# Pools divided by last reader at the two late joints of a hybrid layer, row splits placed among o-projection tiles, and later groups combined on VectorE

## The chip, the cores and the metric

The kernel runs on one core of a Trainium2 chip. The metric is the device time of one execution, in microseconds (us). A core has TensorE (PE), which multiplies matrices into banks of PSUM, VectorE (DVE), ScalarE (ACT) and GpSimd (POOL), each with its own instructions in its own order, and DMA queues that move data between the core's SBUF and the device memory. Engines wait for each other only through semaphores.

## The reference

One layer of a hybrid streaming trunk, for 17 tiles of 128 rows (16 of the prompt, one with eight short streams) and a width of 1024:

```
h   = rmsnorm(x, norm_mix_pre);   P = h @ w_in                    # 1024 x 3592
mix = concat(gated_delta_rule(conv(P[qkv])) * silu(P[z]), P[B] * conv(P[C] * P[H]))
x   = x + rmsnorm(mix @ w_o, norm_mix_post)
h   = rmsnorm(x, norm_ffn_pre)
f   = (silu(h @ w_gate) * (h @ w_up)) @ w_down                    # 1024 x 2816, 2816 x 1024
x   = x + rmsnorm(f, norm_ffn_post)
```

Besides x the layer returns the new convolution caches and the states of the delta rule.

## The kernel before, in words

All products are in fp32, in three passes: each operand is split into a high part that the TensorE format holds exactly and a low part (`xh`/`xl` for the rows, `fw` for gate/up weights, `as` and `dw` in the down projection), and high·high, high·low and low·high are summed in PSUM. A split is a cast on ScalarE (the high part) and a subtraction on VectorE or GpSimd (the low part).

The program has five stages. The **projections** with the delta rule end at about 1028 us. The **o-projection** (`o_tile`, one call for each of 17 tiles) ends at about 1247 us: it loads a tile of mixed rows `mr` and of x (`xo`), splits `mr` into `mh` and `ml`, issues 48 matmuls against `woh`/`wol`, normalizes, adds, normalizes again into `hx` (L731), transposes `hx` with 8 transposes on TensorE (L737), scales them into `ht` (L738) and writes `ht` to the device memory as `hTd` (L741), from where the next stage reads it back.

The **gate/up stage** does 7 products of half-size blocks in place of 8, as Strassen's scheme does. Its rows are in three groups (`FGROUPS`: 6, 6 and 5 tiles). For a group, `ffn_load` reads the row blocks B11 to B22, `ffn_sums` and `ffn_prep` form the combinations T1 to T4 on VectorE and split all seven parts (`PARTS`, four blocks of depth each: 28 casts at L849, 28 subtractions at L850). Before the change the subtractions alternate between VectorE and GpSimd, one for one. Then come 22 rounds, one for each block of 128 hidden columns. A round has weights in seven forms (`gu_weights`, splits at L894 and L895; in group 0 they are computed and mostly stored, later groups load four of the seven), four first products into four PSUM banks (`gu_start`), and `gate_up`: ScalarE copies three banks out into `m1`, `m7`, `m5` (L955 to L957), three further products are added into the banks, VectorE and GpSimd combine them (`u`, `c`, `s7`; L963 to L970), ScalarE applies silu (L966, L971), VectorE multiplies (L983, L984), and every second round ScalarE's queue issues the DMAs that store the six parts for the down projection (`partd`, L995; `lastd`, L987).

The **down projection** runs over five chunks of the hidden columns and eight pairs of row tiles and a single one. `split` (L1059, L1062) prepares `as`, `down_chunk` (L783, L785) prepares `dw`, `product` issues the matmuls (L1078), `evac` and `acc_add` (L1099, L1037) move banks into accumulators. In the last chunk `finish` takes the sum of squares (L1087), the reciprocal root (GpSimd, L130), multiplies by it and by `gpo` (L1092), adds x (L1093) and stores (L1095).

Where code is written in the program order, a list scheduler in the framework decides the order of each engine's instructions from a model of their times. Memory is given out by pools. A pool that is opened over the place of a closed one makes the first writers of its tiles wait for the last readers of what lay there. Around the change the pools are: `op` (all of the o-projection), `fs` (rows of group 0 on load), `fe` (raw weights `rg`, `ru`, sums, 2 split-weight buffers), `fb` (10 more, and the tiles of the epilogue), `fp` (split rows), `fd` and `dr` (loads for the next group, and for the down projection), `dn` (the whole of the down projection). `issue_after` lets a DMA be issued only after a named earlier one. `O_SPLIT` is the number of o tiles that are written ahead of group 0's row splits. Two split weights of the first round lie in closed `woh` tiles (`early`), so that `gu_start` of the first round is written ahead of the closing of `op`.

## Time and profile before

| | |
|---|---|
| median of 3 runs | 2676.9 us (2676.51 to 2684.25) |
| the profiled execution | 2681.64 us, its span 2679.8 us |
| TensorE busy | 2540.3 us, 95% |
| VectorE, ScalarE, GpSimd busy | 1698.4, 945.5, 895.1 us |
| mean granted TensorE clock | 0.976 of full speed |

The span is the time from the first to the last recorded instruction. Busy times can overlap and matmul ends are modelled. A share of busy time is an average over stages with different limits, so the places where TensorE stands idle matter, not the sum. The joints between the stages are at 1152 to 1164 us (row splits of group 0 amid the o-projection), 1256 to 1268 us (o-projection to group 0), 1588 to 1596 us (group 0 to 1), 1912 to 1932 us (group 1 to 2) and 2190 to 2202 us (group 2 to the down projection).

### The profile page before, as it was taken

How to read it: one execution, taken by the hardware profiler on the slowest of the kernel's cores; microseconds unless marked ns; L12 is line 12 of the kernel's file. 1: busy time of each engine (PE TensorE's matmuls, PEld its weight loads, DVE VectorE, ACT ScalarE, POOL GpSimd, SP SyncE). 2: the span in 40 equal slices, each digit the busy share in tenths (PEclk: the TensorE clock that was granted, in tenths of full speed). 3: DMA queues.
4: the chain of work that ended last, by engine and by line, in shares of the span. 5: the costliest groups of instructions: out<-in, count | busy, mean ns of one | idle time of the engine just before them, and what ended most of it. 6: DMA issues, size and time to landing. Idle time of an engine off the chain costs nothing.

```text
span 2679.8 us, 42128 instructions
## 1 busy us (share of the span) xinstructions
PE 2540.3 (95%) x15105; PEld 2358.5 (88%) x15105; DVE 1698.4 (63%) x3405; ACT 945.5 (35%) x2278; POOL 895.1 (33%) x820
## 2 busy tenths in 40 slices
PE   5789999999999999999999999999899999999997
PEld 4679989899898997878999999999899987887775
DVE  7877656576665755586888873433633344777698
ACT  3424134151431513343433442222332335333343
POOL 2221001010000101132655664444544445555563
PEclk8889999999999999999999999999999999999999
DMA  8887655656656565666987777887888853433365
GB/s 297 299 299 264 231 200 197 231 193 217 232 192 218 191 221 173 199 229 211 327 271 268 268 268 251 261 267 243 278 278 277 274 168 109 125 124 120 125 215 175
DMA packets 320241, 602.02 MB, mean 225 GB/s; under 512 B 56876, under 2 KB 206064, under 8 KB 298528
## 3 DMA queue, kind: packets, MB, share of 16 engines
q1 hardware_dynamic: 191728, 522.99, 57.8%
q10 hardware_dynamic: 128304, 76.34, 9.3%
q8 instruction: 119, 1.95, 0.3%
q14 instruction: 90, 0.74, 0.1%
HBM read 437.19 MB, written 162.05 MB: 224 GB/s over the span
## 4 chain that ended last, share of the span: by engine, by line
PE 38%; DVE 6%; issue 2%; POOL 2%; DMA 1%; ACT 1%; ACTq 0%; DVEq 0%; POOLq 0%; SPq 0%
PE fbank L919 28%; PE fbank L1078 10%; DVE xl L850 1%; DVE acc L1037 1%; DVE xr L1093 1%; DVE acc L1092 1%; DMA dr<-in_w_dn 1%; POOL dw L785 1%; DMA fh<-hTd 0%; POOL as L1062 0%; ACTq L995 0%; DVE acc L1125 0%; DVE dw L785 0%; POOL f2r L130 0%; DVE as L1062 0%
## 5 line engine op out<-in xcount | busy, mean ns | idle before, releaser
L919 PE MATMUL fbank<-xh,fw 128*128 128x384 f32 (+1 forms) x3696 | 904.4, 328 | 19.5 <-ACT m L955 10.9
L136 PE MATMUL dbank<-hi,w 128*128 128x384 f32 (+1 forms) x2688 | 705.8, 341 | 33.6 <-ACT w L296 10.4
L919 PEld LDWEIGHTS fbank<-xh,fw 128*128 128x128 f32 x3696 | 655.8, 189 | 22.3 <-ACT m L955 12.4
L919 PE MATMUL fbank<-xl,fw 128*128 128x384 f32 (+1 forms) x1848 | 604.8, 327 | 0.0
L136 PEld LDWEIGHTS dbank<-hi,w 128*128 128x128 f32 x2688 | 494.1, 197 | 47.3 <-ACT w L296 12.0
L1078 PE MATMUL fbank<-dw,as 128*128 128x512 f32 x1980 | 463.9, 395 | 13.0 <-ACT dw L783 4.9
L1078 PEld LDWEIGHTS fbank<-dw,as 128*128 128x128 f32 x1980 | 372.5, 189 | 104.2 <-DVE acc L1037 7.3
L136 PE MATMUL dbank<-lo,w 128*128 128x384 f32 (+1 forms) x1344 | 454.0, 338 | 0.0
L919 PEld LDWEIGHTS fbank<-xl,fw 128*128 128x128 f32 x1848 | 349.3, 189 | 0.0
L136 PEld LDWEIGHTS dbank<-lo,w 128*128 128x128 f32 x1344 | 264.5, 197 | 2.3 <-issue 0.2
L1062 POOL TENSOR_TENSOR as<-ar,as 128x256 fp32r<-128x256 f32 (+1 forms) x207 | 187.6, 916 | 174.2 <-ACT as L1059 170.6
L895 POOL TENSOR_TENSOR fw<-rg,fw 128x512 fp32r<-128x512 f32 x124 | 176.2, 1421 | 181.3 <-ACT fw L894 180.9
L1037 DVE TENSOR_TENSOR acc<-acc,fbank 128x512 f32<-128x512 f32 x248 | 166.5, 682 | 98.7 <-PE fbank L1078 83.1
L1059 ACT CAST as<-ar 128x256 fp32r<-128x256 f32 (+1 forms) x288 | 118.1, 427 | 182.9 <-PE fbank L1078 139.0
L894 ACT CAST fw<-rg 128x512 fp32r<-128x512 f32 x124 | 77.4, 624 | 183.4 <-PE fbank L919 136.9
L508 POOL MEMSET AU<- 32x128 f32 x16 | 3.1, 194 | 409.3 <-PE gbank L494 401.9
L323 DVE SCALAR_TENSOR_TENSOR acc<-R,cw,acc 128x384 f32<-128x384 f32 (+1 forms) x216 | 129.9, 605 | 1.6
L964 POOL TENSOR_TENSOR m<-m,m 128x384 f32<-128x384 f32 (+1 forms) x66 | 69.6, 1055 | 158.3 <-ACT m L957 113.3
L895 POOL TENSOR_TENSOR fw<-ru,fw 128x512 fp32r<-128x512 f32 x62 | 92.4, 1490 | 83.5 <-ACT fw L894 69.0
L963 DVE TENSOR_TENSOR u<-m,fbank 128x384 f32<-128x384 f32 (+1 forms) x66 | 34.8, 528 | 134.4 <-PE fbank L919 127.9
L968 DVE TENSOR_TENSOR c<-u,fbank 128x384 f32<-128x384 f32 (+1 forms) x66 | 34.9, 528 | 127.4 <-PE fbank L919 127.3
L467 DVE TENSOR_TENSOR pr<-As,Ts 48x87 f32<-48x87 f32 (+21 forms) x186 | 64.8, 349 | 30.9 <-DMA As<-sa 26.2
(309 smaller groups left out, 3692.8 us busy)
## 6 DMA issues: line engine op xcount, KB each, us to landing
w<-wsplit SPq DMA_DIRECT2D x140, 1024.0 KB, 4.9
fw<-fsplit SPq DMA_DIRECT2D x188, 512.0 KB, 4.7
fsplit<-fw SPq DMA_DIRECT2D x94, 512.0 KB, 5.3
partd<-pt ACTq DMA_DIRECT2D x88, 384.0 KB, 7.2
rg<-in_w_gu SPq DMA_DIRECT2D x62, 512.0 KB, 3.7
wsplit<-w SPq DMA_DIRECT2D x28, 1024.0 KB, 5.4
ar<-partd SPq DMA_DIRECT2D x48, 384.0 KB, 3.4
ar<-partd SPq DMA_DIRECT2D x64, 256.0 KB, 2.7
```

The lines of the kernel that those rows point to most:

```text
L136: T.matmul(ps, l, r, start=(i == 0), stop=(i == n - 1))
L323: V.scalar_tensor_tensor(acc, raw(d), w[:, d:d + 1], acc, op0=ALU.mult, op1=ALU.add)
L467: V.tensor_mul(p3, As[:m, j, j + 1:32].unsqueeze(2).broadcast_to([m, a, b]), Ts[:m, j, 0:b].unsqueeze(1).broadcast_to([m, a, b]))
L894: A.copy(w[:, 0], v)
L895: e.tensor_tensor(out=w[:, 1], in0=v, in1=w[:, 0].bitcast(F32), op=ALU.subtract)
L919: T.matmul(ps, w_[:, c], b_[k][:, :hw], start=(first and k == 0 and ci == 0), stop=(k == KH - 1 and ci == 2), skip_group_check=not first)
L964: G.tensor_tensor(out=s7, in0=s7, in1=s5, op=ALU.add)
L968: V.tensor_add(c21, u2, b3)
L1037: V.tensor_add(dst, dst, ps)
L1059: ins = A.copy(a[:, 0, :n], v)
L1062: e.tensor_tensor(out=a[:, 1, :n], in0=v, in1=a[:, 0, :n].bitcast(F32), op=ALU.subtract)
L1078: T.matmul(ps, a[:, x_, q * P:(q + 1) * P], w[:, y_], start=(start and q == 0 and ci == 0), stop=(q == c - 1 and ci == 2), skip_group_chec ...
```

## The change

It has six parts.

1. `O_SPLIT` goes from 14 to 8 and `ffn_prep` becomes a generator that yields after each of the seven parts: in program order, group 0's splits of one part are followed by one o tile, seven times, and three o tiles come after.
2. At the joint to group 0, `op` is divided: `oa` holds what the matmuls of the o-projection read (`woh`, `wol`, `mr`, `mh`, `ml`), `op` what the rest of a tile needs. `oa` is closed first and `fb` is opened over it. The two early weights and the early `gu_start` are gone. `NWE`, the weights in `fe`, goes from 2 to 4, and `rg`/`ru` alternate between one buffer in `fe` and one in `fb`.
3. At the joint to the down projection `dn` is divided: `da` (`as`, `ar` and 12 of the `dw` buffers) and `dn` (accumulators and the rest).
4. Groups 1 and 2: the first sums of T2 are computed earlier, with the others (`t2` tiles), and VectorE takes all work that GpSimd had in these rounds: the splits of rows, the splits of three weights (a11, a12, a22) and two additions to `s7`. In group 0 GpSimd keeps one row split of four (`k == 0`).
5. In group 2 the first loads for the down projection (`dr`, `ar0`) are issued after a weight load of that round.
6. `finish` multiplies by `gpo` before the reciprocal root is known, then does one multiply-and-add; for the last tile half of the squares go to VectorE, and its last evacuations get high priority.

```diff
-O_SPLIT = 14
+O_SPLIT = 8
-NWE = 2
+NWE = 4
+NDQ = 12
...
         op = ps_o.enter_context(tc.tile_pool(name="op", bufs=1, reuse_waits="tile", side="right"))
+        oa = ps_a.enter_context(tc.tile_pool(name="oa", bufs=1, reuse_waits="tile", side="right"))
...
-            wh = op.tile([P, D], F32R, name=f"woh{k}")
-            wl = op.tile([P, D], F32R, name=f"wol{k}")
+            wh = oa.tile([P, D], F32R, name=f"woh{k}")
+            wl = oa.tile([P, D], F32R, name=f"wol{k}")
...
-                nc.sync.dma_start(out=t, in_=w_dn[f])
+                with tc.issue_after(wl[0].ins) if not dring else ExitStack():
+                    nc.sync.dma_start(out=t, in_=w_dn[f])
...
-            pool, b = (dr, NDR) if n % NDW < NDR else (dn, NDW - NDR)
+            m = n % NDW
+            pool, b = (dr, NDR) if m < NDR else (da, NDQ) if m < NDR + NDQ else (dn, NDW - NDR - NDQ)
...
+                if gi:
+                    t2.append(fs.tile([P, HW], F32, tag="t2", name="ft2", bufs=KH)[:, :hw])
+                    V.tensor_sub(t2[k], b22, b12)
+                else:
+                    t2.append(b12)
+            return t3, t2
...
-                    (V if k % 2 else G).tensor_tensor(
+                    (G if k == 0 and not gi else V).tensor_tensor(
                         out=l[:, :hw], in0=v, in1=h[:, :hw].bitcast(F32), op=ALU.subtract)
...
-            return X
+                yield X
...
-            hid = ffn_prep(0, hs, ffn_sums(0, hs, fs))
+            prep = ffn_prep(0, hs, ffn_sums(0, hs, fs))
+            for t in range(O_SPLIT, O_SPLIT + len(PARTS)):
+                hid = next(prep)
+                o_tile(t)
...
+            e0 = V if gi else G
...
-            for i, (v, e) in enumerate(((a11, G), (s[2], V), (s[0], G), (s[1], V), (a12, G), (a22, G), (s[3], V))):
+            for i, (v, e) in enumerate(((a11, e0), (s[2], V), (s[0], G), (s[1], V), (a12, e0), (a22, e0), (s[3], V))):
...
-        early += ["woh0", "woh1"]
-        ffetch(2)
-        started = gu_start(0, 0, hid)
+        ps_a.close()
+        fb = ph.enter_context(tc.tile_pool(name="fb", bufs=1, reuse_waits="tile"))
         ps_o.close()
-        fb = ph.enter_context(tc.tile_pool(name="fb", bufs=1, reuse_waits="tile"))
...
-            G.tensor_tensor(out=s7, in0=s7, in1=s5, op=ALU.add)
+            (V if gi else G).tensor_tensor(out=s7, in0=s7, in1=s5, op=ALU.add)
...
-            G.tensor_tensor(out=s7, in0=s7, in1=u2, op=ALU.add)
+            (V if gi else G).tensor_tensor(out=s7, in0=s7, in1=u2, op=ALU.add)
...
+        da = ph.enter_context(tc.tile_pool(name="da", bufs=1, reuse_waits="tile"))
         dn = ph.enter_context(tc.tile_pool(name="dn", bufs=1, reuse_waits="tile"))
...
-                A.activation(junk, v[:, h], AF.Square, accum_out=ss[:, h:h + 1])
+                if h and tail:
+                    V.scalar_tensor_tensor(junk, v[:, h], 1.0, v[:, h], op0=ALU.mult, op1=ALU.mult, accum_out=ss[:, h:h + 1])
+                else:
+                    A.activation(junk, v[:, h], AF.Square, accum_out=ss[:, h:h + 1])
...
             for h in range(2):
+                V.tensor_mul(v[:, h], v[:, h], gpo[:, 512 * h:512 * h + 512])
+            for h in range(2):
                 c = slice(512 * h, 512 * h + 512)
-                V.scalar_tensor_tensor(v[:, h], v[:, h], r, gpo[:, c], op0=ALU.mult, op1=ALU.mult)
-                V.tensor_add(xt[:, c], xt[:, c], v[:, h])
+                V.scalar_tensor_tensor(xt[:, c], v[:, h], r, xt[:, c], op0=ALU.mult, op1=ALU.add)
```

In the built order every engine's instructions are the same up to the o-projection. Three places follow; a row is a line, an operation, its output and input, the shape and a count, and line numbers of the change differ from those of before by 2 to 16 (L860 is L850 of before, L733 is L731).

VectorE in the o-projection, around `hx` of tile 7, which TensorE transposes next. Here `xl` is a low part of a row split, `fh` a row block or a sum of blocks, `oym`, `oxm` and `oss` belong to the norms of o tiles, and `ml` to the split of the next tile. Before:

```order
L128 TENSOR_SCALAR oym<-oss 128x1
L850 TENSOR_TENSOR xl<-ft_12623,xh 128x384
L833 TENSOR_TENSOR fh<-fh 128x384
L850 TENSOR_TENSOR xl<-fh,xh 128x384 x3
L843 TENSOR_TENSOR fh<-fh 128x384
L850 TENSOR_TENSOR xl<-ft_12629,xh 128x384
L731 TENSOR_SCALAR hx<-xo,oyr 128x1024
L843 TENSOR_TENSOR fh<-fh 128x384
L850 TENSOR_TENSOR xl<-fh,xh 128x384
L719 TENSOR_TENSOR oss<-oss 128x1
L709 TENSOR_TENSOR ml<-mr,mh 128x512
```

and with the change:

```order
L129 TENSOR_SCALAR oym<-oss 128x1
L721 TENSOR_TENSOR oss<-oss 128x1
L860 TENSOR_TENSOR xl<-fh,xh 128x384
L711 TENSOR_TENSOR ml<-mr,mh 128x512
L860 TENSOR_TENSOR xl<-fh,xh 128x384
L711 TENSOR_TENSOR ml<-mr,mh 128x512
L853 TENSOR_TENSOR fh<-fh 128x384
L129 TENSOR_SCALAR oxm<-oss 128x1
L853 TENSOR_TENSOR fh<-fh 128x384
L733 TENSOR_SCALAR hx<-xo,oyr 128x1024
L855 TENSOR_TENSOR fh<-fh 128x384
L853 TENSOR_TENSOR fh<-fh 128x384
```

The splits stand in one cluster in both orders (50 rows long before, 58 with the change) and not over seven tiles. VectorE has 21 of the 28 subtractions in place of 14. From the first of them to this `hx` there are 27 rows before and 39 with the change.

ScalarE at the joint of groups 1 and 2. `m` is a bank copied out (L955 to L957 before, L966 to L968 with the change), `c` the silu input, `partd` the stores of the six parts, `fw` a split weight. Before:

```order
L966 ACTIVATE m_19453<-fbank 128x384
L849 CAST xh<-fh 128x320 x9
L971 ACTIVATE c_19456<-c_19456 128x384
L955 COPY m_19643<-fbank 128x320
L956 COPY m_19644<-fbank 128x320
L995 DMA partd_4_117<-pt 128x6x128 x3
L957 COPY m_19645<-fbank 128x320
L894 CAST fw<-rg 128x512
```

and with the change:

```order
L859 CAST xh<-ft_18820 128x320
L859 CAST xh<-fh 128x320 x2
L966 COPY m_19655<-fbank 128x320
L982 ACTIVATE c_19472<-c_19472 128x384
L967 COPY m_19656<-fbank 128x320
L968 COPY m_19657<-fbank 128x320
L907 CAST fw<-rg 128x512
L1006 DMA partd_4_117<-pt 128x6x128 x3
L977 ACTIVATE m_19716<-fbank 128x320
```

The first copy stands ahead of the silu, the third copy and the weight cast ahead of the three stores. All 28 subtractions of this joint are VectorE's, and GpSimd has none.

ScalarE at the joint of group 2 and the down projection. `as` and `dw` are the first operands of it, `ar` and `dr` their sources, `acc` an evacuated bank. Before:

```order
L971 ACTIVATE c_22553<-c_22553 128x320
L987 DMA lastd_127<-pt 128x64
L995 DMA partd_4_122<-pt 128x6x128 x2
L1099 COPY acc_0_22579<-fbank 128x512
L1059 CAST as<-ar 128x256
L783 CAST dw<-dr 128x512 x2
```

and with the change:

```order
L982 ACTIVATE c_22565<-c_22565 128x320
L998 DMA lastd_127<-pt 128x64
L1071 CAST as<-ar 128x256
L787 CAST dw<-dr 128x512 x2
L1071 CAST as<-ar 128x256
L787 CAST dw<-dr 128x512 x2
L1071 CAST as<-ar 128x256
L787 CAST dw<-dr 128x512 x2
L1071 CAST as<-ar 128x256 x2
```

The first casts stand ahead of the stores and of the evacuation, and seven or more of them go before the first evacuation.

On TensorE, at the joint to group 0, 38 o matmuls, 9 product matmuls, 8 transposes, 77 product matmuls and 8 transposes follow each other with the change, where it was 12 o matmuls, 8 transposes, 36 product matmuls and 8 transposes before. In the o-projection 103 o matmuls (up to two tiles ahead) precede the transposes of `hx` above, where it was 79.

More of the change, by code (lines that the diff above doesn't have):

```diff
@@ L753, in fbank @@
         return pool.tile([P, 512], F32, tag=tag, name="fbank")
-    dring, dprep, cast = {}, [], []
+    dring, dprep, cast, wl = {}, [], [], []
     def down_chunk(ch):
@@ L827, in ffn_sums @@
             hw = len(FGROUPS[gi]) * P // 2
-            t3 = []
+            t3, t2 = [], []
             for k in range(KH):
@@ L929, in gu_start @@
             return banks
-        for t in range(O_SPLIT, NT):
+        for t in range(O_SPLIT + len(PARTS), NT):
             if t == NT - 1:
@@ L1002 @@
             if gi:
-                hid = ffn_prep(gi, hs, t3)
+                *_, hid = ffn_prep(gi, hs, t3)
             if gi + 1 < len(FGROUPS):
@@ L1079, in product, with finish @@
                              stop=(q == c - 1 and ci == 2), skip_group_check=True)
-        def finish(v, places):
+        def finish(v, places, tail=False):
             xt = dr.tile([P, D], F32, tag="dr", name="xr", bufs=4)
@@ L1143, in down_single @@
             product(b2, ch, a2, 6, False)
-            evac(c1, b1, ch)
-            acc_add(c2, b2)
-            if ch == len(FCHUNKS) - 1:
+            end = ch == len(FCHUNKS) - 1
+            with tc.high_priority() if end else ExitStack():
+                evac(c1, b1, ch)
+                acc_add(c2, b2)
+            if end:
                 r1, r2 = rows(u)
-                finish(acc[u], [(0, r1), (64, r2)])
+                finish(acc[u], [(0, r1), (64, r2)], True)
         pairs = [(gi, j) for gi, g in enumerate(FGROUPS) for j in range(len(g) // 2)]
```

39 lines of the change are left out of this document (19 added, 20 removed).

## The prediction

> **What bounds the kernel now.** I read the page's totals first, then tables of time windows around each change of stage, then the timeline inside those windows.
>
> ```profile
> span 2679.8 us, 42128 instructions
> PE 2540.3 (95%) x15105; PEld 2358.5 (88%) x15105; DVE 1698.4 (63%) x3405; ACT 945.5 (35%) x2278; POOL 895.1 (33%) x820
> ```
>
> TensorE is busy for 95% of the span, and the change leaves its matmuls as they are. What can be won is the time in which TensorE stands still or runs at a lower granted clock. The windows show where that lies (columns: window in us, its length, busy us and count for each engine, granted TensorE clock, DMA share, GB/s).
>
> ```profile
> core 0: us, PE busy (x) PEld busy (x) DVE busy (x) ACT busy (x) POOL busy (x), PEclk, DMA share, GB/s
> 1152.00:1156.00 4.00, 0.57 (x3) 0.14 (x1) 4.00 (x6) 2.05 (x5) 3.38 (x3) 0.99 0.00 0
> 1156.00:1164.00 8.00, 6.35 (x22) 5.41 (x23) 7.56 (x15) 3.04 (x6) 4.30 (x3) 0.58 0.39 123
> 1256.00:1260.00 4.00, 0.43 (x4) 0.19 (x2) 1.72 (x3) 2.23 (x5) 1.54 (x2) 0.79 0.41 115
> 1260.00:1268.00 8.00, 8.00 (x33) 8.00 (x34) 6.52 (x7) 5.27 (x11) 8.00 (x6) 0.68 0.96 332
> 1588.00:1592.00 4.00, 0.43 (x3) 0.11 (x1) 4.00 (x6) 2.08 (x6) 2.27 (x2) 1.00 0.43 131
> 1592.00:1596.00 4.00, 3.72 (x13) 3.72 (x14) 3.32 (x7) 0.70 (x2) 0.00 (x0) 0.60 0.02 7
> 1912.00:1916.00 4.00, 1.81 (x12) 1.55 (x12) 3.71 (x7) 1.11 (x3) 1.13 (x2) 1.00 0.84 261
> 1916.00:1924.00 8.00, 3.13 (x22) 2.87 (x20) 1.75 (x4) 0.15 (x1) 0.00 (x0) 1.00 1.00 368
> 1924.00:1932.00 8.00, 7.01 (x30) 7.01 (x31) 4.93 (x7) 4.74 (x12) 6.47 (x6) 0.58 0.63 202
> 2190.00:2194.00 4.00, 1.06 (x5) 0.56 (x3) 2.14 (x4) 1.43 (x4) 0.46 (x1) 0.95 0.40 115
> 2194.00:2202.00 8.00, 7.42 (x20) 5.58 (x21) 7.47 (x6) 5.03 (x12) 8.00 (x7) 0.60 0.46 143
> 1264.00:1570.00 306.00, 301.99 (x1732) 300.26 (x1731) 250.06 (x295) 124.50 (x252) 185.95 (x128) 1.00 0.83 289
> 1600.00:1888.00 288.00, 288.00 (x1664) 288.00 (x1663) 108.21 (x147) 80.19 (x159) 120.30 (x101) 1.00 0.81 255
> ```
>
> The two long windows, inside groups 0 and 1, have TensorE full at clock 1.00: nothing can be won there. Each joint loses twice, by idle time and by a low clock just behind it. I count idle as length less PE busy, and clock as PE busy times (1 − clock):
>
> - amid the o-projection: 3.43 + 1.65 idle, 6.35 × 0.42 = 2.67 clock, 7.75 together
> - into group 0: 3.57 idle, 8 × 0.32 = 2.56 clock, 6.1
> - group 0 to 1: 3.57 + 0.28 idle, 3.72 × 0.40 = 1.49 clock, 5.3
> - group 1 to 2: 2.19 + 4.87 + 0.99 = 8.05 idle, 7.01 × 0.42 = 2.9 clock, 11.0
> - into the down projection: 2.94 + 0.58 idle, 7.42 × 0.40 = 2.97 clock, 6.5
>
> That is 36.7 us in five places, the ceiling of the joints. The tail behind the last matmul comes on top.
>
> **The change part by part.** *Amid the o-projection.*
>
> ```profile
> 1156.76 0.74 DVE L731 TENSOR_SCALAR hx<-xo,oyr 128x1024 f32<-128x1024 f32 x1
> 1157.65 1.94 PE L737 MATMUL ftbank<-cst,hx 128*128 128x128 f32 x8 [5.08 <-DVE hx L731]
> ```
>
> TensorE's transposes wait 5.08 us for `hx`, behind a VectorE that is full (4.00 of 4.00): its queue holds the subtractions of the splits. How dear one is depends on GpSimd:
>
> ```profile
> 1577.47 0.55 DVE L843 TENSOR_TENSOR fh<-fh 128x384 f32<-128x384 f32 x1
> 1577.94 1.38 DVE L850 TENSOR_TENSOR xl<-fh,xh 128x384 fp32r<-128x384 f32 x1
> 1577.71 2.48 POOL L850 TENSOR_TENSOR xl<-fh,xh 128x384 fp32r<-128x384 f32 x2 [2.57 <-ACT xh L849]
> ```
>
> Alone such an operation takes 0.55, beside a GpSimd one 1.38, so each subtraction on GpSimd costs VectorE up to 0.83. The change moves 7 of them: VectorE gets 7 × 0.55 = 3.9 more of its own and loses up to 7 × 0.83 = 5.8 of delay. That is 2 better at most on VectorE. Against it, `hx` stands 12 rows later in the cluster; for it, TensorE has 24 more o matmuls ahead of the transposes, at the 6.35 / 22 = 0.29 of the second window some 7 us of cover. The spreading over seven tiles did not happen in the built order. I take 2; bounds −2 (VectorE later, cover used by the rows) to 7.75.
>
> *Into group 0.* The weights of the first round could not be cast until the last tile was through:
>
> ```profile
> 1257.77 0.62 ACT L894 CAST fw<-rg 128x512 fp32r<-128x512 f32 x1 [4.56 <-DVE ht L738]
> ```
>
> ScalarE waits 4.56 us, in order, behind the DMA issue that needs `ht`; TensorE stands 3.57. With `fb` over `oa` alone, these casts and the bank copies need only the o matmuls, and the order has them ahead of that issue; 86 product matmuls fill what 36 did. Against it, round 1's weights are now needed sooner than they are split, since GpSimd is full (8.00 of 8.00) and so are the DMAs (0.96). I put a rest of 1.5 us down for that: 6.1 − 1.5 = 4.6; bounds 2 (a rest as long as today's wait, its clock saved) to 6.1.
>
> *Group 0 to 1.*
>
> ```profile
> 1591.34 0.52 ACT L971 ACTIVATE c<-c 128x384 f32<-128x384 f32 x1 [1.22 <-DVE c L970]
> 1591.77 0.46 ACT L955 COPY m<-fbank 128x384 f32<-128x384 f32 x1
> ```
>
> The bank copy that TensorE waits for is behind a silu, which is behind the `c` addition on a VectorE that is full of splits. In the new order the copy goes first and GpSimd no longer doubles VectorE's operations. The wait goes whole: 5.3; bounds 3.9 (idle only) to 5.3. The later silu is covered by four products.
>
> *Group 1 to 2.* The same wait (2.19) and then a larger one:
>
> ```profile
> 1917.45 6.96 ACTq L995 DMA_DIRECT2D partd<-pt  x3
> 1924.51 0.43 ACT L957 COPY m<-fbank 128x320 f32<-128x320 f32 x1 [8.36 <-issue]
> ```
>
> The third copy stands behind three DMA issues that took 6.96 us while the DMAs were full (share 1.00, 368 GB/s). The change puts copy and weight cast ahead of them, and moves the first 2 MB of down weights to later in the group. What is late next is the first silu behind those issues; its banks are wanted after one product of a round. If the issues still take 7 us, a part comes back. 11.0 less 1.5 = 9.5; bounds 3 (the 2.19, and little more) to 11.0.
>
> *Into the down projection.*
>
> ```profile
> 2191.55 0.97 ACTq L995 DMA_DIRECT2D partd<-pt  x2
> 2194.03 0.80 PE L1078 MATMUL fbank<-dw,as 128*128 128x512 f32 x1 [2.97 <-ACT dw L783]
> ```
>
> TensorE waits 2.97 us for a `dw` cast that stands behind those stores and an evacuation. Now the casts come first, about 2.7 us sooner. But part of the `da` buffers lie over split rows that the last product of group 2 reads, and the low parts behind the casts (GpSimd full, 8.00 of 8.00 in the next window) are unchanged. I take 4 of the 6.5; bounds 0 to 6.5.
>
> How short must a rest be to leave the clock alone? The wait of 2.19 us was followed by a window at 1.00, that of 2.97 by one at 0.60; so I charge no clock to a rest of 1.5. The Trainium skill ("TensorE: Matmul & The Clock Gate", "What's actually happening") halves the clock after an idle window of about 3.4 us, which runs free of the kernel. By that rule the wait of 2.97 could go without a loss, and this last term would be about 2.7 in place of 4, the sum 25.5; the trace shows the loss, so the row decides.
>
> *Tail.*
>
> ```profile
> 2667.53 1.42 DVE L1092 SCALAR_TENSOR_TENSOR acc<-acc,f2r,gpo 128x512 f32<-128x512 f32 x2
> 2668.86 0.68 DVE L1093 TENSOR_TENSOR xr<-xr,acc 128x512 f32<-128x512 f32 x1
> 2669.46 0.68 DVE L1037 TENSOR_TENSOR accs<-accs,fbank 128x512 f32<-128x512 f32 x1
> 2670.24 0.63 ACT L1087 ACTIVATE junkd<-accs 128x512 bf16<-128x512 f32 x1 [5.79 <-DVE accs L1037]
> 2672.82 1.41 DVE L1092 SCALAR_TENSOR_TENSOR accs<-accs,f2r,gpo 128x512 f32<-128x512 f32 x2 [0.73 <-POOL f2r L130]
> 2674.15 1.29 DVE L1093 TENSOR_TENSOR xr<-xr,accs 128x512 f32<-128x512 f32 x2
> ```
>
> Two squares in parallel save about 0.75 (0.63 and its readout). Behind the root stood 1.41 + 1.29 = 2.70; now it is one pass of 1.41, and before it the 1.41 − 0.73 = 0.68 of the multiplication by `gpo` that the wait does not hold: 0.6 less. The last addition, ahead of other tiles' 1.42 + 0.68, can come up to 2.1 sooner, of which I count half. 0.75 + 0.6 + 1.05 = 2.4; bounds 0.5 to 4.
>
> *Costs.* In group 0 VectorE (250.06 of 306) gets four T2 sums for group 1: 4 × 0.55 to 4 × 1.38, 2.2 to 5.5 if nothing hid them; I take −1, bounds −5.5 to 0. In group 1, GpSimd's 101 operations (five a round, at 7 products × 12 = 84 matmuls a round 1664 / 84 = 19.8 rounds) go to VectorE: two of five at 0.55, three on 512 columns at 0.55 × 512/384 = 0.73, about 66 us; 108.21 + 66 = 174 of 288. TensorE's 288.00 hides it: 0. Without that cover it would be 3.3 us a round.
>
> Sum: 2 + 4.6 + 5.3 + 9.5 + 4 + 2.4 − 1 = 26.8. The profiled execution would take 2681.6 − 26.8 = 2654.8. That execution lies 4.7 above the median, so the median goes from 2676.9 to about 2650.
>
> **The rivals.**
>
> *Half of it.* The two joints that depend on VectorE and GpSimd both (amid the o-projection, into group 0) and the down joint give nothing: the first since its splits stay clustered, the others since the split of the next weights ends last anyway. Then 5.3 + 9.5 − 1 + 0.6 of the tail remain, 14.4: about 2662. For it speak GpSimd's full windows behind both joints; against it, that the waits shown end with a ScalarE cast and not with a low part.
>
> *All of it.* Every joint closes and the 24 more o matmuls hide `hx`: 36.7 + 2.4 less 3 of rest, 36, about 2641. Against it speaks the cluster.
>
> *It doesn't do what it says.* Memory decides when loads and splits start, not the readers named: each joint finds another wait of the same length. DMA share 1.00 and the full VectorE are for this; that four of five waits end with a ScalarE instruction placed behind something else is against. Within 8 us of 2676.9.
>
> *Slower: VectorE's order.* With all the work of a later round on VectorE, a subtraction that waits for its ScalarE cast holds the additions behind it, which free the banks.
>
> ```profile
> 2164.81 1.25 DVE L984 TENSOR_TENSOR pt<-m,c 128x320 f32<-128x320 f32 x1 [0.61 <-ACT c L971]
> ```
>
> VectorE already waits for ScalarE (0.61) in a round. It decides when bank readers come later by more than TensorE's run of products, about four of a round's seven: a round is 288 / 19.8 = 14.5 us, so some 8 us. One us over that, in 44 rounds, is 44 us: 2650 + 44 = 2694. Against it: VectorE has 6 us of 14.5 to spare even with the 3.3 more.
>
> **How the numbers follow.** The forecast (2643 to 2657 with its own bounds) gets 0.50, half of it 0.26, all of it 0.11, no effect 0.08, slower 0.05. The joint bounds sum to far more on both sides but won't fall on one side together. The range from 2638 to 2667 takes in the forecast, all, and nearly all of the half case. About 0.3%, 8 us, is what a measurement of this kernel can tell from no change: faster 0.87, same 0.08, slower 0.05.
>
> **What would show it.** Right: the window at the joint of groups 1 and 2 has under 2 us idle and no row in which a bank copy waits for "issue" for several us; group 0 to 1 has no wait of TensorE for the first copy (L966 by then); clock at both stays at 1.00; GpSimd has no busy time in groups 1 and 2, VectorE about 174 of 288, TensorE still 288.00; the last operation on VectorE ends about 2.4 sooner behind the last evacuation's bank than now. Amid the o-projection I expect a wait for `hx` still, of 2 to 5 us. Wrong: TensorE idle inside the rounds of groups 1 and 2; a new wait of TensorE for a low part (`fw` or `dw`) at the start of group 0 or of the down projection; or silu behind stalled stores in group 2's first round.

## The result, and the profile after

The changed kernel takes 2652.99 us (median of 4 runs, 2650.85 to 2655.23), against 2677.15 us before: a ratio of 0.9904, with a 95% interval from 0.9888 to 0.9919. On a second chip the same kernel had 2651.63 against 2682.42 us, 0.9878 (0.9860 to 0.9896). The forecast was 2650, in a range from 2638 to 2667.

The page of the profiled execution (2650.85 us) begins so:

```profile
span 2649.1 us, 41837 instructions
PE 2527.0 (95%) x15105; PEld 2350.1 (89%) x15105; DVE 1755.8 (66%) x3650; ACT 945.3 (36%) x2276; POOL 610.5 (23%) x577
```

TensorE has the same 15105 matmuls and has 13.3 us less of busy time, since it no longer runs at a low clock behind the joints. GpSimd's busy time fell by 285 us.

Single runs of one kernel lie 4 to 12 us apart, about as much as one joint is worth. A sharper measure is how long each stage takes inside a profile, from the first matmul of one stage to that of the next. On the timeline of TensorE, before:

```profile
1028.14 0.47 PE L714 MATMUL dbank<-woh,mh 128*128 128x512 f32 x1
...
1245.74 0.34 PE L919 MATMUL fbank<-xh,fw 128*128 128x384 f32 x1
...
2188.15 0.63 PE L1078 MATMUL fbank<-dw,as 128*128 128x512 f32 x2
...
2662.78 2.34 PE L1078 MATMUL fbank<-dw,as 128*128 128x512 f32 x9
```

and after:

```profile
1029.57 0.48 PE L716 MATMUL dbank<-woh,mh 128*128 128x512 f32 x1
...
1242.95 0.34 PE L932 MATMUL fbank<-xh,fw 128*128 128x384 f32 x1
...
2168.40 0.86 PE L1090 MATMUL fbank<-dw,as 128*128 128x512 f32 x3
...
2627.80 8.38 PE L1090 MATMUL fbank<-dw,as 128*128 128x512 f32 x36
```

The differences of these starts, the end of the last matmul, and the span give the table. It has the same quantities for every kernel that is told of below, each from its own timeline.

| us | o-projection | gate/up | down | tail |
|---|---|---|---|---|
| before | 217.6 | 942.4 | 477.0 | 14.7 |
| changed kernel | 213.4 | 925.5 | 467.8 | 12.9 |
| changed kernel, second profile | 213.2 | 925.2 | 471.3 | 12.9 |
| `b_vector` | 217.6 | 931.1 | 477.8 | 15.0 |
| `u_rows` | 213.5 | 931.9 | 470.2 | 13.5 |
| `u_round` | 216.0 | 920.5 | 469.6 | 12.8 |
| `u_loads` | 213.5 | 924.8 | 470.2 | 12.9 |
| `u_op` | 213.9 | 934.5 | 470.3 | 12.9 |
| `u_dn` | 214.1 | 930.8 | 479.1 | 12.9 |
| `u_split` | 217.3 | 927.9 | 467.9 | 12.8 |
| `u_half` | 221.2 | 928.1 | 467.6 | 12.9 |
| `spread_tail` | 214.0 | 921.6 | 467.9 | 12.2 |
| `spread_tail2` | 214.5 | 922.0 | 468.9 | 12.2 |
| `o_priority` | 225.2 | 936.3 | 469.0 | 12.2 |

The two profiles of the changed kernel agree within 0.3 us, but for the down projection, where they are 3.5 apart. By them the change is worth 4.3 us in the o-projection, 17 in gate/up, 6 to 9 in the down projection and 1.8 in the tail: 29 to 32 together. A stage scatters more than these two profiles show: nine kernels of the table have the same o-projection on TensorE, `u_round` among them, and it takes 213.2 to 216.0 us in them. So one profile does not tell apart less than about 3 us there, nor less than 4 in the down projection. What comes ahead of the o-projection, which the change leaves alone, ends between 1024 and 1035 us in these runs; that is as much as single runs of one kernel lie apart.

The joints of the changed kernel, in windows (columns as in the prediction):

```profile
core 0: us, PE busy (x) PEld busy (x) DVE busy (x) ACT busy (x) POOL busy (x), PEclk, DMA share, GB/s
1152.00:1160.00 8.00, 6.95 (x32) 5.41 (x30) 8.00 (x18) 3.54 (x8) 4.13 (x3) 1.00 0.12 36
1160.00:1168.00 8.00, 5.36 (x28) 4.09 (x27) 8.00 (x16) 3.99 (x10) 1.97 (x2) 1.00 0.36 139
1256.00:1264.00 8.00, 6.70 (x42) 6.41 (x41) 7.49 (x10) 3.29 (x9) 5.19 (x5) 1.00 1.00 391
1264.00:1268.00 4.00, 2.14 (x13) 1.82 (x11) 4.00 (x5) 1.40 (x3) 2.97 (x2) 1.00 0.98 311
1572.00:1580.00 8.00, 8.00 (x48) 8.00 (x47) 8.00 (x18) 4.46 (x10) 0.00 (x0) 1.00 0.81 258
...
1892.00:1900.00 8.00, 8.00 (x55) 8.00 (x54) 7.38 (x18) 4.21 (x10) 0.00 (x0) 1.00 0.82 254
1900.00:1908.00 8.00, 8.00 (x56) 8.00 (x55) 3.72 (x9) 1.38 (x4) 0.00 (x0) 1.00 0.95 309
2032.00:2036.00 4.00, 4.00 (x29) 4.00 (x28) 0.40 (x1) 0.00 (x0) 0.00 (x0) 1.00 1.04 410
2036.00:2040.00 4.00, 0.68 (x5) 0.41 (x4) 1.01 (x2) 1.66 (x4) 0.00 (x0) 1.00 0.35 125
2168.00:2176.00 8.00, 6.68 (x26) 4.18 (x25) 6.76 (x8) 5.95 (x15) 5.00 (x4) 1.00 0.36 107
2176.00:2184.00 8.00, 5.90 (x25) 4.52 (x25) 8.00 (x9) 4.16 (x9) 8.00 (x7) 1.00 0.45 141
...
1600.00:1860.00 260.00, 260.00 (x1502) 260.00 (x1501) 129.81 (x228) 73.04 (x143) 0.00 (x0) 1.00 0.80 257
```

The two joints between groups (near 1576 and 1896 us now) are gone: TensorE is full across them, at clock 1.00. The other three are about halved. One loss is new: in 2036 to 2040, inside group 2, TensorE is busy for 0.68 of 4 us. It is in the round in which the first loads for the down projection now stand. On ScalarE and TensorE:

```profile
2028.69 0.62 ACT L787 CAST dw<-dr 128x512 fp32r<-128x512 f32 x1 [0.79 <-DMA dr<-in_w_dn]
2037.41 0.34 ACTq L998 DMA_DIRECT2D lastd<-a  x1
...
2038.34 0.62 ACT L907 CAST fw<-rg 128x512 fp32r<-128x512 f32 x1 [9.03 <-DMA partd<-pt]
...
2039.69 0.42 PE L932 MATMUL fbank<-xh,fw 128*128 128x320 f32 x1 [3.32 <-ACT m L966]
```

ScalarE stood idle for 9.03 us ahead of this cast, behind the small store `lastd`, while the DMAs were full (share 1.04, 410 GB/s), and the next bank copy came late. The row names what ended the wait: an earlier store, `partd`, landed. Each DMA of this program reports its landing on one of eight semaphores, and before it is issued its queue waits until the DMA that last used the same one has landed. In the trace's semaphore records `lastd` shares one with the second `partd` store, which was issued at 2021.36, beside the 2 MB of loads, and landed at 2037.34; `lastd` followed at 2037.41, and its own issue took 0.34 us. So it is another stall than that of the joint of groups 1 and 2 before, where the issue of the third store itself took 5.8 of the 6.96 us.

### The profile page after: what moved, and what is told of

The parts are those of the page before. It is cut to its first block, busy times and chain, and to the rows that moved or that the text cites. A ratio compares the mean times of both kernels' runs of the same rounds, so it can differ in the third digit from the quotient of the medians.

```text
span 2649.1 us, 41837 instructions
## 1 busy us (share of the span) xinstructions
PE 2527.0 (95%) x15105; PEld 2350.1 (89%) x15105; DVE 1755.8 (66%) x3650; ACT 945.3 (36%) x2276; POOL 610.5 (23%) x577
## 4 chain that ended last, share of the span: by engine, by line
PE 70%; DVE 13%; DMA 9%; ACT 3%; issue 3%; POOL 1%; SPq 0%; ACTq 0%; DVEq 0%; POOLq 0%
PE fbank L932 30%; PE dbank L137 20%; PE fbank L1090 10%; PE tbank L716 2%; PE dbank L716 2%; DVE acc L324 1%; DMA w<-wsplit 1%; DVE xr L1109 1%; DMA wr<-in_w_in 1%; DVE acc L1049 1%; DMA dt<-grow 1%; DMA hTd<-ht 1%; DMA partd<-pt 1%; DMA grow<-rw 1%; PE gbank L448 1%
## 5 line engine op out<-in xcount | busy, mean ns | idle before, releaser
L789 POOL TENSOR_TENSOR dw<-dr,dw 128x512 fp32r<-128x512 f32 x52 | 76.9, 1493 | 483.5 <-ACT dw L787 483.2
L975 DVE TENSOR_TENSOR m<-m,m 128x384 f32<-128x384 f32 (+1 forms) x44 | 23.1, 526 | 83.6 <-ACT m L968 83.6
L977 ACT ACTIVATE m<-fbank 128x384 f32<-128x384 f32 (+1 forms) x66 | 31.3, 474 | 126.3 <-PE fbank L932 118.7
L908 POOL TENSOR_TENSOR fw<-rg,fw 128x512 fp32r<-128x512 f32 x44 | 69.7, 1583 | 28.3 <-ACT fw L907 28.1
```

Of the source, the lines that this page charges most:

```text
L789: e.tensor_tensor(out=w[:, 1], in0=v, in1=w[:, 0].bitcast(F32), op=ALU.subtract)
L908: e.tensor_tensor(out=w[:, 1], in0=v, in1=w[:, 0].bitcast(F32), op=ALU.subtract)
```

## The experiments

Each but `b_vector` starts from the changed kernel. "Lost" is idle time plus clock, as in the prediction.

**Row splits of later groups on both engines (`u_rows`).**

```diff
-                    (G if k == 0 and not gi else V).tensor_tensor(
+                    (G if (k % 2 == 0 if gi else k == 0) else V).tensor_tensor(
```

> The changed kernel with one thing undone: in groups 1 and 2 the subtractions of the row splits alternate between VectorE and GpSimd again (14 and 14). T2's early sums, the weights' splits and the additions to s7 stay on VectorE. Theory A (engines): the joints of groups 0-1 and 1-2 closed because GpSimd no longer doubles VectorE's operations (0.55 to 1.38 us); then TensorE's wait for the first bank copy comes back at both, 5.3 us at the first (3.85 idle and its clock) and 2.2 at the second: about 2653 + 7 = 2660. Theory B (sums and order): the joints closed because T2's first sums were made earlier and the bank copies go ahead of the silu; then both joints stay under 1 us idle and the time stays at 2653.

Measured: 2658.41 us, 0.9919 (0.9902 to 0.9936); gate/up 6.4 us longer than in the changed kernel. VectorE at the joint of groups 0 and 1, and its window:

```profile
1575.42 0.55 DVE L855 TENSOR_TENSOR ft<-fh,ft 128x384 f32<-128x384 f32 x1
1575.89 1.38 DVE L860 TENSOR_TENSOR xl<-fh,xh 128x384 fp32r<-128x384 f32 x1
```

```profile
1580.00:1584.00 4.00, 1.59 (x9) 1.27 (x8) 3.41 (x6) 1.14 (x3) 0.73 (x1) 1.00 0.44 140
```

The operations double again, 0.55 to 1.38, and TensorE waits 2.41 us for the first bank copy there and 0.88 for the third: 3.3 lost where the changed kernel loses nothing. So the engine of the row splits decides at this joint, as theory A has it. By which way is not told apart, since the edit also put ScalarE's order back:

```profile
1582.11 0.52 ACT L982 ACTIVATE c<-c 128x384 f32<-128x384 f32 x1 [3.94 <-DVE c L981]
1582.54 0.46 ACT L966 COPY m<-fbank 128x384 f32<-128x384 f32 x1
```

The silu stands ahead of the first copy again, and three stores ahead of the third. ScalarE idled 3.94 us for the silu's operand `c`, which VectorE made late, while TensorE had finished the four first products at 1580.64. In the changed kernel's order the copy would not have waited for `c`. At the joint of groups 1 and 2 only 0.7 us came back, so there something else counts.

**Weights' splits and `s7` on GpSimd (`u_round`).**

```diff
-            e0 = V if gi else G
+            e0 = G
```

and the two additions to `s7` likewise.

> The changed kernel with the splits of three weights and the two additions to s7 on GpSimd again in groups 1 and 2; the row splits there stay on VectorE. Theory A: TensorE hides this work on either engine inside a round, and at the joints it is the row splits' engine that counts; both joints stay under 1 us idle, 2653. Theory B: GpSimd beside VectorE in the joint's last and first rounds doubles the row splits as well; a wait for the first bank copy of 2 to 3.5 us comes back at each joint, 2653 + 5.

Measured: 2650.39 us, 0.9881 (0.9865 to 0.9898), where the changed kernel had 0.9878 on the same chip. Both joints stay whole; theory A holds. Gate/up is 5 us shorter: the stall in round 10 of group 2 does not happen, TensorE is full from 2024 to 2044. There the store `lastd` was issued at 2029.80, 1 us after the cast, and not 9. The traces show why: here `lastd` shares its semaphore with the first of the loads, which had landed, and not with the second `partd` store, which landed at 2036.22, about as long after its issue as in most of the others. The 2 MB stand in this round all the same. In all seven kernels of the table that have the wait in round 10, both profiles of the changed kernel counted, the two stores share a semaphore; in the five others that start from the changed kernel they do not. Which DMAs share one follows from the order in which all of them are issued.

**The loads for the down projection at the joint again (`u_loads`).**

```diff
-                with tc.issue_after(wl[0].ins) if not dring else ExitStack():
-                    nc.sync.dma_start(out=t, in_=w_dn[f])
+                nc.sync.dma_start(out=t, in_=w_dn[f])
```

and the same for `ar0`.

> The changed kernel with the first down loads (2 MB) and ar0 issued without waiting for a weight load, so that they stand at the joint of groups 1 and 2 again; the bank copies and the weight cast stay ahead of the stores. Theory A (collision): the 7 us in which ScalarE's queue could not issue its stores came from these loads, and with them back the stall is back; the copies are ahead of it, so the first silu of group 2 is what is late, TensorE stands some 3 to 5 us idle at the joint with a low clock behind it, and the 3.3 us idle that the changed kernel has ten rounds later, where the loads now lie, is gone: 2653 + (5 to 8) - 3.3, about 2656. Theory B (order): the stall hurt only because the third copy stood behind it; the joint stays under 1 us idle and the round ten later is whole: 2653 - 3.3 = 2650.

Measured: 2649.12 us, 0.9894 (0.9876 to 0.9912); gate/up 0.6 shorter than in the changed kernel. ScalarE at the joint of groups 1 and 2, and TensorE after it:

```profile
1902.78 5.41 ACTq L1005 DMA_DIRECT2D partd<-pt  x2
1908.29 0.44 ACT L976 ACTIVATE m<-fbank 128x320 f32<-128x320 f32 x1 [5.26 <-issue]
...
1914.13 0.42 PE L931 MATMUL fbank<-xh,fw 128*128 128x320 f32 x1 [2.18 <-ACT m L965]
```

The stall is back, 5.41 us of issuing, as theory A has it. But the bank copies and the weight cast are ahead of it, so TensorE loses 2.2 us and not the 11 of before, and the 3.3 of round 10 is saved. The time is theory B's 2650, though the joint does not stay under 1 us. So what closed this joint in the main is the order on ScalarE; that the loads were moved brought nothing, the two losses being within 1.2 us of each other.

**VectorE's part alone (`b_vector`).** The kernel before with part 4 of the change and nothing else.

> The kernel before with the fourth part of the change alone: in groups 1 and 2 VectorE does all row splits, the splits of three weights and the additions to s7, and T2's first sums are made early. Group 0, the pools, the loads for the down projection and the tail are as before. Theory A (this part alone closes the two joints between groups): the losses of 5.3 and 10.9 us there fall to under 2 together, the other joints stay as they were (8.0 amid the o-projection, 6.2 into group 0, 10 into the down projection): 2677.5 - 14 = 2663.5. Theory B (the later loads are needed for the joint of groups 1 and 2): that joint keeps some 8 us of its loss: about 2671. Either way no idle time of TensorE inside the rounds.

Measured: 2671.26 us, 0.9963 (0.9949 to 0.9978), which is 10 us; gate/up 11.3 shorter, the other stages as before. The window of the joint of groups 0 and 1 is full, and at that of 1 and 2 ScalarE and the window show:

```profile
1908.64 0.63 ACT L901 CAST fw<-rg 128x512 fp32r<-128x512 f32 x1
...
1912.89 6.21 ACTq L1002 DMA_DIRECT2D partd<-pt  x2
```

```profile
1920.00:1932.00 12.00, 9.78 (x56) 9.52 (x55) 10.57 (x17) 5.34 (x12) 4.55 (x3) 0.86 0.94 291
```

The stores stall as before (6.21), but the cast and all three copies are now ahead of them: the scheduler has changed ScalarE's order because VectorE's work changed. The loss of 16.3 us at the two joints falls to 2.2 idle and 1.4 clock. That is between the theories, 3.6 where A said under 2 and B some 8, and so is the time, 10 us against 14 and 6.5. Part 4 alone does close the most of both joints, with a rest as in `u_loads`.

**The pool of the o-projection in one piece (`u_op`).**

```diff
-        oa = ps_a.enter_context(tc.tile_pool(name="oa", bufs=1, reuse_waits="tile", side="right"))
+        oa = op
...
         ps_a.close()
-        fb = ph.enter_context(tc.tile_pool(name="fb", bufs=1, reuse_waits="tile"))
         ps_o.close()
+        fb = ph.enter_context(tc.tile_pool(name="fb", bufs=1, reuse_waits="tile"))
```

> The changed kernel with the pool of the o-projection in one piece again, the new weight buffers opened over it when it is closed (no early weights, four weights in the other pool as in the change). Theory A (pools): the joint to group 0 lost 6.1 us before and loses about 3 in the changed kernel because the weights' buffers no longer wait for xo, hx and ht of the last tiles; here the casts stand behind the last tile's ht again, TensorE idles about 3.5 us in one piece with a low clock behind it: 2653 + 3 to 5, about 2657. Theory B: the joint gained by more product matmuls in reserve (86 for 36) and four weights fetched ahead, which stay: 2653.

Measured: 2660.07 us, 0.993 (0.9915 to 0.9945); gate/up 9 us longer than in the changed kernel. ScalarE and TensorE into group 0:

```profile
1254.42 0.62 ACT L907 CAST fw<-rg 128x512 fp32r<-128x512 f32 x1 [4.61 <-DVE ht L740]
```

```profile
1256.50 0.69 PE L932 MATMUL fbank<-xh,fw 128*128 128x384 f32 x1 [3.57 <-ACT m L966]
```

That is the wait of before, to the hundredth: 3.57 us, and 3.1 of clock behind it, 6.7 in place of the 3.3 of the changed kernel. Theory A holds. Another 4.9 us are lost at 1320 to 1328, where ScalarE's next bank copy came 4.80 us late, behind three stores; the undivided pool is the only edit, but by which way it led there was not followed.

**The pool of the down projection in one piece (`u_dn`).**

```diff
-        da = ph.enter_context(tc.tile_pool(name="da", bufs=1, reuse_waits="tile"))
         dn = ph.enter_context(tc.tile_pool(name="dn", bufs=1, reuse_waits="tile"))
+        da = dn
```

and all `dw` buffers but the first four in `dn`.

> The changed kernel with the down projection's pool in one piece again (accumulators, as, ar and all dw buffers behind the same closed pools). Theory A (pools): the first as and dw casts wait for the last readers of the gate/up epilogue again, behind the last stores and the evacuation; TensorE's wait of about 3 us with the low clock behind it comes back: 6.5 lost in place of 3.2 at that joint, about 2653 + 3.5 = 2656.5. Theory B: what made this joint shorter is GpSimd, which comes to it with nothing left of group 2 to do; then it stays at 3.2 and the time at 2653.

Measured: 2660.42 us, 0.9935 (0.9919 to 0.9951); the down projection 8 to 11 us longer (479.1, where it was 477.0 before the change). ScalarE and TensorE there:

```profile
2172.82 0.59 ACT L1115 COPY acc<-fbank 128x512 f32<-128x512 f32 x1 [3.15 <-issue]
```

```profile
2174.28 0.50 PE L1090 MATMUL fbank<-dw,as 128*128 128x512 f32 x1 [2.90 <-ACT dw L787]
...
2204.36 8.03 PE L1090 MATMUL fbank<-dw,as 128*128 128x512 f32 x23 [2.20 <-DVE acc L1049]
```

The evacuation is ahead of the casts again, and the wait for `dw` is back (2.90). Theory A holds, and the price is two to three times what it said, since the delay is paid again 30 us later, where TensorE waits 1.52 and 2.20 us. Gate/up is 5 us longer too: 4.4 idle in place of 3.3 in round 10, and 1.4 to 1.7 of clock at each of three places where the changed kernel's first profile lost none.

**The row splits written after 14 tiles (`u_split`), and 14 of them on GpSimd (`u_half`).**

```diff
-O_SPLIT = 8
+O_SPLIT = 14
...
-            for t in range(O_SPLIT, O_SPLIT + len(PARTS)):
-                hid = next(prep)
-                o_tile(t)
+            *_, hid = prep
```

> The changed kernel with the row splits of group 0 written after 14 o tiles, as before, and not one part ahead of each of seven tiles; GpSimd keeps the 7 subtractions of the change in place of 14. Theory A (order): the gain amid the o-projection, 8.0 lost before and 3.6 with the change, comes from the o matmuls that the new program order lets TensorE do ahead; then about 8 is lost again, 2653 + 4 = 2657. Theory B (engines): it comes from GpSimd's 7 fewer operations beside VectorE; then 3.6 stays and so does 2653.

```diff
-                    (G if k == 0 and not gi else V).tensor_tensor(
+                    (G if k % 2 == 0 and not gi else V).tensor_tensor(
```

> The changed kernel with 14 of group 0's 28 subtractions on GpSimd again, and the new program order kept. Theory A (order): the loss amid the o-projection stays at 3.6, 2653. Theory B (engines): VectorE's operations double beside GpSimd, the loss there goes back to about 8: 2653 + 4 = 2657.

Measured: 2657.84 us, 0.9914 (0.9894 to 0.9934), and 2659.38 us, 0.9916 (0.9893 to 0.9938). The o-projection takes 217.3 us in the first, 3.9 more than in the changed kernel and what it took before; in the second it takes 221.2, 7.8 more. TensorE in `u_split`:

```profile
1154.30 1.88 PE L739 MATMUL ftbank<-cst,hx 128*128 128x128 f32 x8 [1.97 <-DVE hx L733]
...
1165.03 0.76 PE L716 MATMUL dbank<-woh,mh 128*128 128x512 f32 x1 [3.03 <-DVE xo L726]
```

The wait for `hx` is back, and the one for a bank (`xo`, 2.6 in the changed kernel) is there too. So theory A fits the first kernel and theory B the second: each half of part 1 is needed. For `u_half` that is clear. `u_split` is only 1.3 us above the longest of the nine kernels with the change's o-projection, and of its 3.9 us about 1.3 are idle time and the rest low clock behind the two waits. In `u_half` VectorE is busy for 29.69 of the 30 us from 1140, with 48 operations against the changed kernel's 59: it does fewer and takes as long.

**Loads spread over four rounds, and a scrap tile of its own (`spread_tail`, `spread_tail2`).** In the changed kernel's tail VectorE shows why its square did not run beside ScalarE's:

```profile
2638.97 0.68 DVE L1049 TENSOR_TENSOR accs<-accs,fbank 128x512 f32<-128x512 f32 x1
2640.50 0.69 DVE L1100 SCALAR_TENSOR_TENSOR junkd<-accs 128x512 bf16<-128x512 f32 x1 [0.85 <-ACT junkd L1102]
...
2643.27 1.42 DVE L1109 SCALAR_TENSOR_TENSOR xr<-accs,f2r,xr 128x512 f32<-128x512 f32 x2 [0.73 <-POOL f2r L131]
```

It waits for ScalarE, since both write `junkd`, a tile that nobody reads.

```diff
-                    V.scalar_tensor_tensor(junk, v[:, h], 1.0, v[:, h], ...
+                    V.scalar_tensor_tensor(junk2, v[:, h], 1.0, v[:, h], ...
...
-                    prep_step(2)
-                elif 10 < f <= 10 + NDR:
+                    prep_step(1)
+                elif 10 < f <= 13 + NDR:
```

with a `yield` behind each of the first four loads.

> The changed kernel with two things added. The four first down loads (0.5 MB each) are issued in four rounds, one after a weight load of each, in place of all in one round. In the tail the square on VectorE writes a scrap tile of its own, since in the changed kernel it waited 0.85 us for ScalarE's square, which writes the same one. Theory A (collision): the 3.3 us in round 10 of group 2 come from 2 MB at once before ScalarE's stores, and one load per round leaves no wait over 0.5 us; with some 0.7 us off the tail 2653 - 4 = 2649. Theory B: the stall comes with any of these loads, since the stores queue behind them whatever their number: a wait of about 1 us in each of four rounds, 2652.

Measured: 2645.43 us, 0.987 (0.9846 to 0.9894). Then once more, beside the changed kernel:

> The changed kernel once more, on the same chip as the next ones. Both theories: ratio to the kernel before 0.988 to 0.992. Which windows of low clock follow the waits of 3 to 4 us that are left (amid the o-projection, into group 0, round 10 of group 2) is expected to differ from the first profile, where none did, if the clock depends on where a wait falls in a window of its own; under the other reading, that waits under 3.5 us leave the clock alone, none does again.

> The changed kernel with the first down loads one in a round and a scrap tile of its own for the square, once more, beside the changed kernel on the same chip. Theory A (the two waits that this takes away, 3.3 and about 0.7 us, are its whole gain): 4 us below the changed kernel, a ratio of 0.9985 to it. Theory B (the larger difference between the two in the calls so far, 0.9870 to 0.9904, is real): 8 to 9 us.

Measured: 2651.63 us for the changed kernel, 2650.26 for this one, 0.9879 (0.9861 to 0.9897). The stages show what the medians can't: gate/up takes 921.6 and 922.0 us in place of 925.5 and 925.2, the tail 12.2 in place of 12.9 both times. VectorE's square and round 10 to 11 of group 2 in `spread_tail`:

```profile
2634.45 0.68 DVE L1103 SCALAR_TENSOR_TENSOR junke<-accs 128x512 bf16<-128x512 f32 x1
```

```profile
2020.00:2040.00 20.00, 20.00 (x139) 20.00 (x138) 8.92 (x18) 6.23 (x15) 1.61 (x1) 1.00 0.88 304
```

The square waits for nobody and TensorE is full. Theory A's 4 us are there, in both profiles. That spreading the loads is what closed round 10 is not shown: here too `lastd` does not share its semaphore with the second `partd` store, which still took 13.3 and 14.3 us to land (15.2 and 16.0 in the changed kernel). That the whole kernel is faster for it is not shown, the two medians being 1.4 apart and each uncertain by some 5.

**o tiles at high priority (`o_priority`).** On top of that, `with tc.high_priority():` around the seven o tiles.

> spread_tail with the seven o tiles among which the row splits of group 0 are written given high priority in the scheduler. Theory A (the cluster of splits on VectorE ahead of the tile's norm chain is what TensorE waits for amid the o-projection): the chain goes first, the idle time there falls from 3.5 us to under 1.5. Theory B (the chain's own length, from the last matmul of a tile over its squares, roots and products to its transposes, is what TensorE waits for once its banks are full): it stays at 3 us or more wherever the splits stand.

Measured: 2672.74 us in its one run, the o-projection 225.2. Theory A fell, and theory B's 3 us or more is met in number only: there is now one wait of 15.46 us for the bank of a tile (`xo`), and what the priority did to VectorE's order ahead of it was not followed up. It shows that more than the order of splits and chain counts there, and nothing on how to gain.

## Why the prediction was right, point by point

**The sum.** Forecast −26.8; the medians give −24.2 and, on the second chip, −30.8, the stages 29 to 32. It is the forecast case, between 2643 and 2657, and no rival: the half case needed the joint to group 0, the down joint and the o-projection to give nothing, and each gave 2.8 us or more. That the sum comes so close is in part luck: the terms for groups 1 to 2 and into group 0 were 1.8 too high each, those amid the o-projection and into the down projection too low by 2.3 and by 1.7 or more.

**Group 0 to 1** (5.3 forecast): 5.3. The wait went whole. `u_rows` shows that the engine of the row splits decides. The prediction gave two reasons, the copy ahead of the silu and operations on VectorE that no longer double beside GpSimd; `u_rows` turns both back and does not tell them apart.

**Group 1 to 2** (9.5): the loss of 11 is gone there, and 3.3 came back in round 10. The mechanism was right in one half: the copies and the cast ahead of the stores are what counts (`b_vector`, `u_loads`). The other half, that moving the loads helps, is not borne out: `u_loads` has them at the joint again and loses no more. What came back in round 10 is a store's wait for an earlier store that shares its semaphore, which no page of before could show. I named the silu behind stalled stores as the thing to watch, but at the joint, and put down only 1.5.

**Into group 0** (4.6): 2.8, from 6.1 to 3.3 in both profiles. The rest is not the start of round 1's weights that I put 1.5 down for. TensorE waits 1.30 us for the last tile's `hx` and 1.99 for its `ht`: the end of the o-projection now lies among product matmuls and holds them up, since VectorE has sums and splits of weights ahead of it. `u_op` gives back the old wait.

**Amid the o-projection** (2): 4.3, or 1.6 to 4.4 over the nine kernels with the same o-projection. Too low, but inside its bounds. I took the two edits as alternatives and expected a wait for `hx` of 2 to 5 us. None over 0.3 us is left in the first profile; what is left is 1.05 for `ml` and 2.64 for a bank. `u_split` and `u_half` show that the cover of the 24 more matmuls and the seven fewer operations on GpSimd are needed together.

**Into the down projection** (4): 5.7 to 9.2, of which 2 to 3.5 may be scatter. The term was mis-sized because I counted the loss only up to 2202 us. Before, TensorE lost more at 2204 to 2208 and 2216 to 2224, from the same delay; `u_dn` has such a second payment, 30 us behind the first.

**Tail** (2.4): 1.8. Of the 0.75 for squares in parallel nothing came, because of the shared scrap tile; with its own, 12.2 and so 2.5.

**VectorE in later groups** (0, at 174 of 288): TensorE is full, so 0 holds; but VectorE is busy for 129.81 of 260, or 144 of 288. The added work was 36 and not 66. That fits operations that no longer double beside GpSimd: the mean of all was 0.74 us (108.21 / 147) and is 0.57 (129.81 / 228). The slower rival had less to stand on than I thought. T2's early sums in group 0 (−1) cannot be told from nothing: `b_vector` has them and its gate/up gained 11.3, where the two joints lost 12.7 less. The window inside group 0 that the prediction calls full was not: 301.99 of 306. The changed kernel waits there too, 2.07 us at 1390 and 1.67 at 1411, so some 4 us were passed over.

**The clock.** I charged none to short rests and all to a wait of 2.97. That step is wrong as a rule, though it cost the sum little: no wait of the changed kernel's first profile, up to 3.32 us, cost any clock, and one of 1.43 in `spread_tail2` did (below).

## What to carry to other kernels

Where one engine's queue carries bank copies, casts and store issues, ask of each joint which of them TensorE needs first; a change of engine for some other work can reorder that queue through the scheduler and gain as much as the work itself, here some 7 of the 11 us of `b_vector`. When a copy is late behind a store, look at what the store waited for: its own issue, or the landing of an earlier DMA with which it shares a semaphore. The second kind comes and goes with edits elsewhere, as in `u_round`. And compare stages by the first matmul of each: that told apart 0.7 us in the tail, where medians of four runs could not tell 4. Kernels that share a stage show how far it scatters.

## What was not expected of the hardware

The granted clock does not follow from the length of a wait. In the clock records of these traces it is 1.00 or 0.50, and it changes only at the borders of pieces of 3.41 us. The same joint into group 0, with the same pair of waits on TensorE (1.3 for `hx`, 2.0 for `ht`, 3.3 idle together), in the second profile of the changed kernel and in `spread_tail2`, cut at these borders:

```profile
1262.55:1265.96 3.41, 2.58 (x15) 2.26 (x14) 3.41 (x4) 1.83 (x5) 3.21 (x2) 1.00 0.94 261
1265.96:1269.37 3.41, 2.25 (x13) 2.25 (x14) 3.37 (x6) 0.63 (x2) 0.41 (x2) 1.00 1.03 413
```

```profile
1272.26:1275.67 3.41, 1.44 (x9) 1.19 (x8) 3.41 (x6) 0.00 (x0) 1.15 (x1) 1.00 0.98 399
1275.67:1279.09 3.42, 3.42 (x12) 3.42 (x11) 2.80 (x5) 2.55 (x6) 1.28 (x1) 0.50 1.02 352
```

In the first the wait of 2.0 lies across a border, TensorE is busy for 2.58 and 2.25 us of the two pieces, and the clock stays at 1.00. In the second it lies inside one piece, TensorE is busy for 1.44 of it, and the next piece runs at 0.50, which loses up to 1.7 us. Round 10 is alike: the wait of 3.32 us in the first profile of the changed kernel left 1.52 and 1.98 us busy on its two sides and cost no clock, the wait of 2.56 in the second left 0.85 of one piece and cost a piece at 0.50. From 1031 to 2630 us the first profile has no piece at 0.50 and the second has three: amid the o-projection behind the same 2.64 us, in round 10, and in the down projection at 2351.

Over all fourteen profiles in that stretch, all 36 pieces at full clock in which TensorE was busy for less than 43% are followed by one at 0.50, and none of some 6400 with 55% or more. Of the 34 between, 7 are; one of them holds the wait of 1.43 us in the last chunk of the down projection of `spread_tail2` (1.77 of 3.42 busy). So what counts is how much of one piece the waits take away. The borders lie elsewhere in each run (at 1263.43 in the changed kernel's first profile, at 1262.55 in its second), so to the kernel a wait of 1.4 to 3.6 us remains a chance of losing up to 1.7 us. The Trainium skill ("TensorE: Matmul & The Clock Gate", "What's actually happening") has the window that decides run free of the kernel and gives it about 3.4 us, which agrees with this; that the window must be idle does not, with low clock behind pieces in which TensorE was busy for up to 42%, and behind some with 51 to 54%.
